# Turning the first half of the gated mixer sum by transposing DMAs in 16-bit halves, in place of TensorE transposes

## The chip, the core and the metric

The kernel runs on one core of one Trainium2 chip. The metric is the device time of one execution in microseconds (us), as the median of several runs. The core has five engines with queues of their own, which meet only through semaphores: TensorE (PE; its weight loads are shown as PEld), VectorE (DVE), ScalarE (ACT), GpSimd (POOL) and SyncE (SP). SP and POOL issue the transfers of this kernel, and an engine's instructions, issues included, run in the order of its own queue.

## The reference

It is an encoder of two layers over 512 tokens of 1024 channels, in float32. Each layer is a gated feed-forward half step, a mixer of two parallel branches, and a second feed-forward half step. The change touches the mixer's end:

```python
z = h @ w_in                                     # q, k, v, uf, ga, gf
y_na = neighbourhood_attention(q, k, v, rpb) @ w_na_out
y_f = fourier_mix(uf) @ w_f_out
g_na = jax.nn.sigmoid(ga + gate_bias[0])
g_f = jax.nn.sigmoid(gf + gate_bias[1])
return (g_na * y_na + g_f * y_f) @ w_o
```

The gated sum in brackets is 512 tokens x 1024 channels. To multiply it by `w_o`, the kernel needs it with channels on the partitions, while the gates produce it with tokens on the partitions. So it has to be turned.

## The kernel before

**Products.** Every large product is one Strassen step: both operands are cut in quarters, and seven products replace eight (numbered m; in the gate blocks their order is 1, 5, 2, 6, 7, 3, 4). Each float32 operand is split into a high part of few mantissa bits (`whi`, `xh`) and the rest (`wlo`, `xl`), and each product of two tiles is three matmuls: high by high, high by low, low by high (lines L491, L492, L494). A product works over two granules of weights (128 x 1024 float32, 512 KB each) and writes two PSUM banks (`A`, `B`, `C`), one for each 128 tokens. For each granule a raw load arrives by DMA (`raw`, L148 from SP's queue, L150 and L196 from POOL's queue, which add a second granule in memory), ScalarE rounds it to `whi` (L191, L186), and VectorE takes the difference `wlo` (L194, L187). Three buffers of `whi` and of `wlo` exist, so the rounding of a granule waits until TensorE has left the granule three before it. Eight granules are fetched ahead.

**Buffers.** In the mixer nearly all tiles of 4 KB a partition (raw weights, products taken out of PSUM, gated sums, turned tiles) come from one ring of 23 slots (`slot`, L111). A load into a slot waits for the last reader of the tile that was there.

**The gate blocks.** `gate_block(i, ...)` (L1371) computes both gates for column half i (512 of the 1024 channels) and all tokens, in the order of `ORDER`, and adds both gated branches. After m = 1 and m = 5 the results are evicted from PSUM by ScalarE (`snap`, L561, tile `sn`, one instruction for each bank); after m = 6 the product in the banks of `A` is evicted a second time, and m = 7 adds into the same two banks. A dictionary `after` names a function that is called behind a product. Block 0 leaves its sum in `ga0`, two tiles (j = 0, 1, 256 tokens each) of two token blocks of 512 channels. Block 1 runs next; it needs nothing of `ga0`, and its dictionary calls the turning of `ga0`, which is wanted only behind block 1 (`m00`, `m01`).

**Turning before the change.** `to_channels(i, ga, j)` (L1452) takes one tile in two steps. Each step makes four TensorE transposes of 128 x 128 float32 (L1459) into one PSUM bank and one ScalarE eviction (L1460) into the turned tile `mq`. It is called for j = 1 behind m = 5 and for j = 0 behind m = 2 of block 1, in each of the two layers; block 1's own sum is turned by the same function later and is not touched.

**A second way of turning that the kernel has.** The feed-forward stages turn their tile `z` of the same size by DMA (`halves` and `joined`, L676 to L698). A transposing DMA moves elements of 16 bits, so ScalarE first copies the low and the high 16-bit words into a tile `zs` (two copies, L681), one transposing DMA on SP's queue turns `zs` into `zt` (L682), and ScalarE later joins the words again into 32-bit elements (L698).

**Order of the queues.** A scheduler places the instructions of each engine by estimated times; in blocks under `manual_schedule` an engine keeps the order in which the code is written. In `gate_block` that is the case for ScalarE around the eviction behind m = 6:

```python
elif m == 6:
    product(pa, acts[6], K4, False, again=True)
    with tc.manual_schedule(engines={mybir.EngineType.Activation}):
        s2 = snap(pa)
        with_n(arg(s1, 0, 0), 0)
```

Of the kernel before, what the change touches and what calls it, by code (L numbers as in the profile page):

```python
# [9 lines left out]
F32 = mybir.dt.float32  # L10
# [3 lines left out]
U16 = mybir.dt.uint16  # L14
AF = mybir.ActivationFunctionType
# [3 lines left out]
P = 128  # L19
# [71 lines left out]
def encoder_kernel(  # L91
    ctx: ExitStack, tc: tile.TileContext, xin, xtr, wst, gains, gfin, gbias, bias_in, dft, chan, ident_in, rot, out
):
    nc = tc.nc
    V, S, G, PE = nc.vector, nc.scalar, nc.gpsimd, nc.tensor
# [11 lines left out]
    def nm(s):  # L107
        uid[0] += 1
        return f"{s}_{uid[0]}"

    def slot(dt=F32, s="k", shape=(4, 256)):  # L111
        return kp.tile([P, *shape], dt, tag="k", name=nm(s), bufs=23)
# [5 lines left out]
    def bank(s="ps"):  # L118
        return pp.tile([P, T], F32, tag="ps", name=nm(s))

    def pair(s="ps"):
        return [bank(s), bank(s)]
# [208 lines left out]
    def rsqrt(ms, n):  # L331
# [6 lines left out]
            V.scalar_tensor_tensor(r, t, 1.5, r, ALU.add, ALU.mult)  # L338
        return r

    class Norm:


# [214 lines left out]
    def snap(ps):  # L558
        t = slot(F32, "sn", (2, T))
        for b in range(2):  # L560
            S.activation(t[:, b, :], ps[b], AF.Copy)  # L561
        return t

    def less(ps, t):
        for b in range(2):
            res = V.tensor_tensor(t[:, b, :], ps[b], t[:, b, :], ALU.subtract)  # L566
        return res

    def combos(norm, t4):


        norm.tiles(0)
        norm.tiles(1)
        raw, hx, lx = norm.raw, norm.h, norm.l
        acts = {1: (hx[0], lx[0], 0), 2: (hx[1], lx[1], 0), 3: (hx[1], lx[1], 256)}
        if t4:
            acts[4] = (*t4, 0)

        def combine(m):
            p, a, b, op = {  # L580
                5: ((0, 0), (0, 0), (0, 1), ALU.subtract),
                7: ((0, 1), (0, 1), (1, 1), ALU.subtract),
                6: ((0, 0), (1, 1), (0, 0), ALU.add),
                4: ((1, 0), (1, 0), (0, 0), ALU.subtract),
            }[m]
            V.tensor_tensor(raw[p], raw[a], raw[b], op)
            yield
            if m != 4 or not t4:
                acts[m] = (slot(F32R, f"t{m}h"), slot(F32R, f"t{m}l"), 0)
            h, l, _ = acts[m]  # L590
            S.activation(h, raw[p], AF.Copy)
            yield
            V.tensor_tensor(l, raw[p], h.bitcast(F32), ALU.subtract)
            yield

        return acts, combine

    def stage_ffn(norm, nxt, late):
# [4 lines left out]
        def at_tile(h, j, c):  # L603
            if (h, j, c) not in at:
                at[h, j, c] = slot(F32, "at")
            return at[h, j, c]
# [35 lines left out]
        acts, steps_of = combos(norm, t4)  # L642
# [6 lines left out]
        if first:  # L649
            for g in range(2):  # L650
                w = ws.next()
# [22 lines left out]
        late_at, turned = [], []  # L674

        def halves(z, j, f0):  # L676

            s, t = slot(U16, "zs", (2, 4, 2, P)), slot(U16, "zt", (2, 4, 256))
            words = z.bitcast(U16).rearrange("p b (q f h) -> p h q b f", q=4, h=2)
            for h in range(2):  # L680
                S.activation(s[:, h], words[:, h], AF.Copy)  # L681
            nc.sync.dma_start_transpose(  # L682
                out=t.rearrange("p h q (b t) -> p (h q b) t", b=2), in_=s.rearrange("p h q b f -> p (h q b f)")
            )
            turned.append((t, j, f0))

        def joined():

            t, j, f0 = turned.pop(0)
            q = 0  # L690
            while q < 4:
                h, c, i = PLACE[f0 + q]
                n = 1
                while q + n < 4 and PLACE[f0 + q + n] == (h, c, i + n):
                    n += 1
                to = at_tile(h, j, c).bitcast(U16).rearrange("p i (t w) -> p w i t", w=2)
                for w in range(2):
                    S.activation(to[:, w, i : i + n, :], t[:, w, q : q + n, :], AF.Copy)  # L698
                q += n

        def plain_out():
# [161 lines left out]
        for jb in range(0 if first else 1, NB):  # L863
            f0 = 2 + 4 * jb
            if first and jb == 0:
                with tc.manual_schedule(engines={mybir.EngineType.DVE, mybir.EngineType.Activation}):
                    pa = pair("A")
                    product(pa, acts[1], K4, True)
                    for j in range(2):
                        t = snap(pcl[j])  # L870
# [13 lines left out]
            if turned:  # L884
                joined()
# [149 lines left out]
    def stage_mixer(l, norm, nxt):  # L1035
# [181 lines left out]
        def four_ch(b):  # L1217
            bh, bl = b
            p1, p2 = bank(), bank()
            mm3(p1[:, 0:258], ch[:, 0, 0, :], ch[:, 0, 1, :], bh[:, 0:258], bl[:, 0:258], True, True)  # L1220
            mm3(p2[:, 0:256], ch[:, 1, 0, :], ch[:, 1, 1, :], bh[:, 256:512], bl[:, 256:512], True, True)
            return p1, p2
# [27 lines left out]
        o, q, k, bms = [], {}, {}, {}  # L1250
# [120 lines left out]
        def gate_block(i, bias, acts, after):  # L1371

            r = norm.r

            def arg(src, which, j):
                t = src if src is not None else slot(F32, "ga", (2, T))
                for b in range(2):
                    c = 2 * j + b
                    V.scalar_tensor_tensor(
                        t[:, b, :], pa[b] if src is None else t[:, b, :], r[:, c : c + 1],  # L1380
                        bias[which][:, i * T : (i + 1) * T], ALU.mult, ALU.add,
                    )
                S.activation(t, t, AF.Tanh, scale=0.5)
                return t

            def gated(t, y):
                V.scalar_tensor_tensor(y, t, 1.0, y, ALU.add, ALU.mult)

            done = []

            def both(j):

                if j in done and (i, j) in ns:
                    V.tensor_tensor(fs[i, j], fs[i, j], ns[i, j], ALU.add)
                done.append(j)

            def with_f(t, j):
                gated(t, fs[i, j])
                both(j)

            def with_n(t, j):
                if (i, j) in ns:
                    gated(t, ns[i, j])
                    both(j)
                else:
                    ga[j] = t

            ga = [None, None]
            for m in ORDER:
                if m == 1:  # L1410
                    pa = pair("A")
                    product(pa, acts[1], K4, True)
                    s1 = snap(pa)
                elif m == 5:
                    pb = pair("B")
                    product(pb, acts[5], K4, True)
                    sb = snap(pb)
# [5 lines that stand above are left out]
                elif m == 2:  # L1423
                    pc = pair("C")
                    product(pc, acts[2], K4, True)
                    less(pc, s1)
                elif m == 7:
                    product(pa, acts[7], K4, False, again=True)
                    less(pa, sb)
                    with_f(arg(sb, 1, 1), 1)  # L1430
                elif m == 3:
                    product(pb, acts[3], K4, False, again=True)
                    less(pb, s2)
                    with_n(arg(s2, 0, 1), 1)
                else:
                    product(pa, acts[4], K4, False, again=True)
                    with_f(arg(None, 1, 0), 0)
                if m in after:
                    after[m]()
            return ga if (i, 0) not in ns else [fs[i, 0], fs[i, 1]]  # L1440
# [9 lines left out]
        mq = {}  # L1450

        def to_channels(i, ga, j):  # L1452
            mq[i, j] = slot(F32, "mq")
            for q in range(2):
                tr = bank("tr").rearrange("p (a b) -> p a b", a=2)
                for k in range(2):
                    for b in range(2):
                        d = (2 * q + k) * P
                        PE.transpose(tr[:, k, b * P : (b + 1) * P], ga[j][:, b, d : d + P], ident)  # L1459
                S.activation(mq[i, j][:, 2 * q : 2 * q + 2, :], tr, AF.Copy)  # L1460
# [26 lines left out]
        with tc.manual_schedule(engines={mybir.EngineType.DVE, mybir.EngineType.Activation}):  # L1487
            with tc.manual_schedule(engines={mybir.EngineType.PE}):
# [29 lines left out]
                f0, f1 = four_ch(b_[0]), four_ch(b_[1])  # L1518
# [26 lines left out]
                for s in range(3):  # L1545
                    t = slot(F32, "vs", (T,))
# [134 lines left out]
        acts = {1: (hx[0], lx[0], 0), 2: (hx[1], lx[1], 0), 3: (hx[1], lx[1], 256), 4: (hx[0], lx[0], 256)}  # L1681
# [11 lines left out]
        with tc.manual_schedule(engines={mybir.EngineType.DVE, mybir.EngineType.Activation}):  # L1693
# [10 lines left out]
            w = [ws.next(), ws.next()]  # L1704
        for _ in fill(o, ns, 0, w):
            pass
        bias = []
# [20 lines left out]

        ga0 = gate_block(0, bias, acts, {1: third_parts, 6: fourth})

        ga1 = gate_block(1, bias, acts, {5: lambda: to_channels(0, ga0, 1), 2: lambda: to_channels(0, ga0, 0)})
        m00, m01 = mq[0, 0], mq[0, 1]
        a1 = parts(m00, "m1")
        a5 = combo(m00, m00, m01, ALU.subtract, "m5")
        w = [ws.next(), ws.next()]
# [233 lines left out]
```

## Time and profile before

| | |
|---|---|
| median of 3 runs | 1862.26 us (1861.38 to 1863.63) |
| profiled execution, its own time | 1859.98 us |
| its span on the core | 1858.2 us |
| mean granted clock of TensorE in it | 0.998 |
| instructions | 24666 |
| busy: TensorE / VectorE / ScalarE | 99% / 86% / 70% of the span |
| mean transfer over the span | 211 GB/s |

The second gate block lies at about 516 to 556 us of the span in the first layer and at about 1437 to 1476 us in the second.

The page gives, in this order: the busy time of each engine; the span in 40 slices; the DMA queues; the chain of work that ended last, followed back from the last instruction to whatever released each step; and the costliest groups of instructions. A row of the order of time has the start (us from the span's start), the length, the engine, the line of the kernel, the operation, the tiles (out<-in), the shape and the count. In brackets stands the idle time of the engine just before it and what ended that. Engine names with a q (SPq) are queue entries that issue transfers. Neighbouring matmuls overlap, so their pace is read from start to start and not from their lengths. A row of a view by tile has the least, median and greatest length in ns, and the first and last start.

### The profile page before, as it was taken

What the parts mean: (1) busy time and instruction counts of PE and PEld (TensorE: products, weight loads), DVE (VectorE), ACT (ScalarE), POOL (GpSimd) and SP (SyncE); (2) the same over time, 40 slices, a digit from 0 to 9 for tenths busy, and PEclk for the clock granted to TensorE, in tenths of its full rate; (3) what the DMA queues carried; (4) which work ended last, traced back from release to release, by engine and by line L of the source; (5) the groups of instructions that cost most, each with busy time, mean ns of one, the idle gap of its engine ahead of it and who ended that gap; (6) DMA issues with size and microseconds to landing.
All of it is one profiled execution on the core that took longest, in us unless ns stands there. A gap on an engine that the chain in (4) does not pass through costs nothing.

```text
span 1858.2 us, 24666 instructions
## 1 busy us (share of the span) xinstructions
PE 1843.7 (99%) x8894; PEld 1533.9 (83%) x8894; DVE 1606.6 (86%) x1950; ACT 1300.2 (70%) x1772; POOL 171.3 (9%) x210
## 2 busy tenths in 40 slices
PE   9999999999999999999999999999999999999997
PEld 7888888888888888888888888888888888888886
DVE  7878899786989987889998888997869899888899
ACT  6777875668665767777666778666676576777865
POOL 0001011100101000101001100101001101010010
PEclk9999999999999999999999999999999999999999
DMA  9898799942986788879889897989249867998794
GB/s 302 223 232 218 198 256 274 213 121 86 254 219 164 171 227 231 208 200 264 256 194 223 224 221 199 269 278 209 69 149 236 210 171 176 229 215 215 210 280 148
DMA packets 190139, 392.13 MB, mean 211 GB/s; under 512 B 95488, under 2 KB 95616, under 8 KB 190016
## 3 DMA queue, kind: packets, MB, share of 16 engines
q1 hardware_dynamic: 161344, 292.20, 49.8%
q0 software_dynamic: 28528, 98.33, 30.2%
q8 instruction: 70, 1.15, 0.3%
q14 instruction: 53, 0.43, 0.1%
q10 hardware_dynamic: 144, 0.02, 0.0%
HBM read 365.85 MB, written 2.11 MB: 198 GB/s over the span
## 4 chain that ended last, share of the span: by engine, by line
PE 97%; DVE 1%; ACT 1%; DMA 0%; issue 0%; SPq 0%; DVEq 0%
PE A L491 10%; PE A L492 10%; PE A L494 10%; PE o L492 7%; PE o L494 7%; PE o L491 7%; PE B L492 5%; PE B L491 5%; PE B L494 5%; PE ps L315 4%; PE ps L316 3%; PE ps L317 3%; PE C L492 3%; PE C L491 3%; PE C L494 3%; PE tr L396 1%
## 5 line engine op out<-in xcount | busy, mean ns | idle before, releaser
L194 DVE TENSOR_TENSOR wlo<-raw,whi 128x1024 fp32r<-128x1024 f32 (+1 forms) x534 | 632.4, 1194 | 172.2 <-ACT whi L191 170.9
L191 ACT ACTIVATE whi<-raw 128x1024 fp32r<-128x1024 f32 (+1 forms) x534 | 547.4, 1033 | 265.6 <-PE A L492 58.5
L150 POOL DMA_DIRECT2D raw<-in_wst_dram x166 | 144.2, 885 | 1335.0 <-DMA raw<-in_wst_dram 794.1
L164 DVE TENSOR_TENSOR raw<-raw,raw 128x1024 f32<-128x1024 f32 (+1 forms) x150 | 179.2, 1195 | 2.0
L492 PE MATMUL A<-whi,xl 128*128 128x512 f32 x400 | 155.9, 390 | 0.0
L491 PE MATMUL A<-whi,xh 128*128 128x512 f32 x400 | 155.8, 390 | 0.0
L698 ACT ACTIVATE at<-zt 128x1024 uint16<-128x1024 uint16 (+2 forms) x96 | 111.0, 1169 | 20.9 <-DMA zt<-zs 20.9
L186 ACT ACTIVATE whi<-raw 128x1024 fp32r<-128x1024 f32 (+1 forms) x83 | 85.8, 1035 | 49.6 <-issue 12.5
L494 PE MATMUL A<-wlo,xh 128*128 128x512 f32 x400 | 115.1, 389 | 0.0
L187 DVE SCALAR_TENSOR_TENSOR wlo<-raw,whi 128x1024 fp32r<-128x1024 f32 (+1 forms) x83 | 98.4, 1195 | 13.7 <-ACT whi L186 13.7
L494 PEld LDWEIGHTS A<-wlo,xh 128*128 128x128 f32 x400 | 75.1, 188 | 15.6
L491 PEld LDWEIGHTS A<-whi,xh 128*128 128x128 f32 x400 | 75.1, 188 | 15.4
L492 PEld LDWEIGHTS A<-whi,xl 128*128 128x128 f32 x400 | 75.2, 188 | 15.3
L722 ACT ACTIVATE th<-sn,rh 128x512 f32<-128x512 f32 x80 | 55.2, 716 | 37.7 <-DVE sn L566 36.8
L491 PE MATMUL C<-whi,xh 128*128 128x512 f32 x208 | 81.2, 390 | 0.0
L492 PE MATMUL B<-whi,xl 128*128 128x512 f32 x208 | 81.1, 390 | 0.0
L492 PE MATMUL C<-whi,xl 128*128 128x512 f32 x208 | 81.0, 390 | 0.0
L491 PE MATMUL B<-whi,xh 128*128 128x512 f32 x208 | 81.0, 390 | 0.0
L681 ACT ACTIVATE zs<-th 128x1024 uint16<-128x1024 uint16 x80 | 79.5, 1043 | 0.7 <-DVE th L729 0.7
L561 ACT ACTIVATE sn<-A 128x512 f32<-128x512 f32 x104 | 59.1, 585 | 24.9 <-PE A L494 24.9
L494 PE MATMUL B<-wlo,xh 128*128 128x512 f32 x208 | 59.9, 390 | 0.0
L494 PE MATMUL C<-wlo,xh 128*128 128x512 f32 x208 | 59.8, 390 | 0.0
(438 smaller groups left out, 4676.5 us busy)
## 6 DMA issues: line engine op xcount, KB each, us to landing
raw<-in_wst_dram SPq DMA_DIRECT2D x470, 512.0 KB, 5.8
raw<-in_wst_dram POOLq DMA_DIRECT2D x174, 512.0 KB, 7.9
raw<-in_wst_dram SPq DMA_DIRECT2D x30, 256.0 KB, 4.1
bm<-in_bias_dram SPq DMA_DIRECT2D x16, 384.0 KB, 3.5
x<-in_xin_dram SPq DMA_DIRECT2D x4, 512.0 KB, 10.2
raw<-in_wst_dram POOLq DMA_DIRECT2D x8, 256.0 KB, 8.2
dft<-in_dft_dram POOLq DMA_DIRECT2D x8, 256.0 KB, 4.5
gb<-in_gbias_dram SPq DMA_DIRECT2D x4, 512.0 KB, 15.6
```

Of the source, the lines that this page charges most:

```text
L150: G.dma_start(out=self.t, in_=wst[GRAN_AT[self.plus]][:, 0 : self.n], accum_op=ALU.add)
L164: V.tensor_tensor(self.raw.t, self.raw.t, self.add.t, ALU.add)
L186: S.activation(hi, t, AF.Copy, scale=-1.0)
L187: self.last = V.scalar_tensor_tensor(lo, t, -1.0, hi.bitcast(F32), ALU.mult, ALU.subtract)
L191: S.activation(hi[:, cs], t[:, cs], AF.Copy)
L194: self.last = V.tensor_tensor(lo[:, cs], t[:, cs], hi[:, cs].bitcast(F32), ALU.subtract)
L315: PE.matmul(ps, lh, rh, start=start, stop=False, skip_group_check=again)
L491: PE.matmul(ps, lh, rh, start=start, stop=False, skip_group_check=again)
L492: PE.matmul(ps, ll, rh, start=False, stop=False, skip_group_check=again)
L494: PE.matmul(ps, lh, rl, start=False, stop=stop, skip_group_check=again)
L681: S.activation(s[:, h], words[:, h], AF.Copy)
L698: S.activation(to[:, w, i : i + n, :], t[:, w, q : q + n, :], AF.Copy)
```

## The change

The body of `halves` becomes a function `apart` and the joining of words becomes `joined_words`; the feed-forward stages call them with the same work as before. In the second gate block of the mixer, `ga0` is turned with them. Behind m = 1 the tile j = 1 is split and its transposing DMA issued, behind m = 5 the tile j = 0. Behind m = 2 the words of j = 1 are joined into `mq`, and behind m = 7 those of j = 0. The 2 x 8 TensorE transposes and 2 x 2 evictions of each layer go; 2 x 2 splitting copies, 2 transposing DMAs and 2 x 2 joining copies of each layer come. Two tiles for each turned tile, `zs` and `zt`, take slots of the ring.

In the built program the rest keeps its order on each engine but for a few neighbours in the block. The splits stand on ScalarE between and behind the two evictions of m = 1 and of m = 5, ahead of the weights. The first copy of the second join stands between the two evictions behind m = 6, the second behind the next weight rounding. On TensorE the first granule of m = 7 takes both banks' high-weight matmuls first and the low-weight ones behind them; before, the first bank's two low-weight matmuls stood between. On SP the two transposing DMAs have two weight loads between them. On VectorE the sum of two raw granules and the last addition of block 0 move ahead of one `wlo`.

```diff
+    def apart(z):
+
+        s, t = slot(U16, "zs", (2, 4, 2, P)), slot(U16, "zt", (2, 4, 256))
+        words = z.bitcast(U16).rearrange("p b (q f h) -> p h q b f", q=4, h=2)
+        for h in range(2):
+            S.activation(s[:, h], words[:, h], AF.Copy)
+        nc.sync.dma_start_transpose(
+            out=t.rearrange("p h q (b t) -> p (h q b) t", b=2), in_=s.rearrange("p h q b f -> p (h q b f)")
+        )
+        return t
+
+    def joined_words(to, t):
+
+        to = to.bitcast(U16).rearrange("p i (t w) -> p w i t", w=2)
+        for w in range(2):
+            S.activation(to[:, w], t[:, w], AF.Copy)
...
-        ga1 = gate_block(1, bias, acts, {5: lambda: to_channels(0, ga0, 1), 2: lambda: to_channels(0, ga0, 0)})
+        turned = {}
+
+        def taken(j):
+            turned[j] = apart(ga0[j])
+
+        def channels(j):
+            mq[0, j] = slot(F32, "mq")
+            joined_words(mq[0, j], turned[j])
+
+        ga1 = gate_block(
+            1, bias, acts, {1: lambda: taken(1), 5: lambda: taken(0), 2: lambda: channels(1), 7: lambda: channels(0)}
+        )
```

More of the change, by code (lines that the diff above doesn't have):

```diff
@@ L676, in halves @@
         def halves(z, j, f0):
[L678 to L685, printed above, removed]
+            turned.append((apart(z), j, f0))
         def joined():
@@ L695, in joined @@
                     n += 1
-                to = at_tile(h, j, c).bitcast(U16).rearrange("p i (t w) -> p w i t", w=2)
-                for w in range(2):
-                    S.activation(to[:, w, i : i + n, :], t[:, w, q : q + n, :], AF.Copy)
+                joined_words(at_tile(h, j, c)[:, i : i + n, :], t[:, :, q : q + n, :])
                 q += n
```

## The prediction

> **What bounds the kernel now.** First the page: the span, the busy shares, the chain that ended last. Then the tile that the removed transposes write, then the order of time of TensorE and ScalarE in the second gate block of the first layer, then the waits and stretches around it.
>
> ```profile
> span 1858.2 us, 24666 instructions
> PE 1843.7 (99%) x8894; PEld 1533.9 (83%) x8894; DVE 1606.6 (86%) x1950; ACT 1300.2 (70%) x1772; POOL 171.3 (9%) x210
> ...
> PE 97%; DVE 1%; ACT 1%; DMA 0%; issue 0%; SPq 0%; DVEq 0%
> ```
>
> TensorE is busy in 99% of the span and carries 97% of the chain. So an instruction taken off TensorE is worth its whole pace, and anything added elsewhere costs only what it makes TensorE wait. The view of stretches for the block in both layers (us busy and number of instructions of TensorE, its weight loads, VectorE, ScalarE and GpSimd, then granted clock, DMA share and GB/s):
>
> ```profile
> 521.00:528.00 7.00, 7.00 (x34) 5.78 (x34) 7.00 (x7) 4.77 (x7) 0.00 (x0) 1.00 0.29 82
> 528.00:534.00 6.00, 6.00 (x31) 5.00 (x30) 4.96 (x6) 3.24 (x6) 1.67 (x2) 1.00 0.97 264
> ...
> 521.00:556.00 35.00, 35.00 (x163) 29.00 (x163) 29.11 (x31) 21.93 (x27) 3.44 (x4) 1.00 0.82 212
> 1441.00:1476.00 35.00, 35.00 (x163) 29.00 (x162) 29.12 (x32) 21.78 (x27) 3.44 (x4) 1.00 0.78 213
> ```
>
> TensorE has no gap in either layer, at full granted clock. The second layer repeats the first (163 matmuls and 27 ScalarE instructions in 35 us in each), so I cost one layer and double it. ScalarE has 13 us free of 35. The DMA engines are at 0.29 up to 528 and at 0.97 behind it.
>
> **What the removal is worth.** The order of time on TensorE around the two groups of eight transposes:
>
> ```profile
> 527.16 0.62 PE L494 MATMUL B<-wlo,t1h 128*128 128x512 f32 x2
> 527.62 1.04 PE L1459 MATMUL tr<-ident,fs 128*128 128x128 f32 x8
> 528.41 0.48 PE L491 MATMUL C<-whi,xh 128*128 128x512 f32 x1
> 528.73 0.40 PE L492 MATMUL C<-whi,xl 128*128 128x512 f32 x1
> ...
> 533.50 0.62 PE L494 MATMUL C<-wlo,xh 128*128 128x512 f32 x2
> 533.96 1.03 PE L1459 MATMUL tr<-ident,fs 128*128 128x128 f32 x8
> 534.75 0.48 PE L491 MATMUL A<-whi,t2h 128*128 128x512 f32 x1
> 535.06 0.39 PE L492 MATMUL A<-whi,t2l 128*128 128x512 f32 x1
> ```
>
> The pace of the products is 0.23 us (two matmuls from 527.16 to 527.62). A group costs its own 0.79 us (527.62 to 528.41), and the product's first matmul behind it takes 0.32 us in place of 0.23. That is 0.88 us a group, the second one the same (0.79 and 0.31). Two groups in each of two layers: 4 x 0.88 = **3.54 us** off the path. These are all 32 transposes of the change.
>
> **What is added, and where it stands.** Each of the two tiles now takes two ScalarE copies into 16-bit halves, one transposing DMA on SP's queue, and two ScalarE copies that join the words, in place of two ScalarE evictions. The same steps stand in the feed-forward stages, on tiles of the same size, so they have prices:
>
> ```profile
> L681 ACT ACTIVATE zs<-th x80: 1035/1042/1063, 70.6 to 1748.8; 128x1024 uint16<-128x1024 uint16 x80
> L698 ACT ACTIVATE at<-zt x96: 477/1358/1386, 83.7 to 1767.1; 128x1024 uint16<-128x1024 uint16 x64, 128x256 uint16<-128x256 uint16 x16, 128x768 uint16<-128x768 uint16 x16
> L682 SPq DMA_TRANSPOSE zt<-zs x40: 1359/3700/7223, 72.6 to 1750.3; - x40
> DMA to landing us min/median/max: 4.3/5.9/10.1
> L1460 ACT ACTIVATE mq<-tr x16: 578/592/604, 528.8 to 1495.8; 128x512 f32<-128x512 f32 x16
> ```
>
> ScalarE gains 4 x 1.04 + 4 x 1.36 - 4 x 0.59 = 7.2 us in each layer, against 13 us free: it fits, if nothing urgent stands behind. ScalarE now, in order of time (tiles: whi the rounded weights, sn the products taken out of PSUM):
>
> ```profile
> 521.44 0.58 ACT L561 ACTIVATE sn<-A 128x512 f32<-128x512 f32 x1
> 521.97 1.06 ACT L191 ACTIVATE whi<-raw 128x1024 fp32r<-128x1024 f32 x1
> 533.75 1.06 ACT L191 ACTIVATE whi<-raw 128x1024 fp32r<-128x1024 f32 x1 [2.11 <-PE C L492]
> 539.12 0.60 ACT L561 ACTIVATE sn<-A 128x512 f32<-128x512 f32 x1 [1.21 <-PE A L494]
> 540.03 1.06 ACT L191 ACTIVATE whi<-raw 128x1024 fp32r<-128x1024 f32 x1 [0.31 <-PE A L492]
> 541.00 0.58 ACT L561 ACTIVATE sn<-A 128x512 f32<-128x512 f32 x1
> ```
>
> In the changed program the order is: sn, zs, sn, zs, whi, whi, sn, zs, sn, zs, whi, whi, both copies of the first join, whi, whi, sn, a copy of the second join, sn, the gate's tanh, whi, the last copy. I lay them end to end from 521.44, at 0.53 us from an eviction's start to the next step's (521.44 to 521.97) and 0.97 for a copy of 1.04 or 1.06 us (540.03 to 541.00). The splits end at 524.5 and 529.5, and the transposes are issued there. The weights that now start at 521.97 start at 524.4 and are ready at 525.5. They belong to the product that starts at 528.41 and will start at 527.5, so 2 us are left, and TensorE loses **nothing**. Without that cover it would lose up to the 2.4 us by which they moved. The first join stands at 531.3 to 533.9 and asks for a landing within 6.8 us of the issue. It starts while the DMA engines are at 0.29, where the range's lower half, 4.3 to 5.9, fits. Behind it stand the weights now at 533.75, wanted at 540.28 less 1.77, 538.5. They start at 533.9 and have 3.5 us left: **nothing** again.
>
> **The place that costs.** The second join's first copy stands between the two evictions of the product for m = 6, and the next product, m = 7, writes the same two banks again:
>
> ```profile
> 540.28 0.39 PE L491 MATMUL A<-whi,t3h 128*128 128x512 f32 x1
> ...
> 541.19 0.62 PE L494 MATMUL A<-wlo,t3h 128*128 128x512 f32 x2
> 541.64 0.48 PE L491 MATMUL A<-whi,t3h 128*128 128x512 f32 x1
> 541.96 0.40 PE L492 MATMUL A<-whi,t3l 128*128 128x512 f32 x1
> ```
>
> Here TensorE already loses 0.09 us (541.64 to 541.96 where 0.23 is the pace), because its seventh matmul needs the bank that the eviction at 541.00 to 541.58 frees. In the changed program that matmul stands fifth: the two low-weight matmuls that filled the time are moved behind it. So the bank is wanted 0.45 us sooner. The same three ScalarE steps stand in a feed-forward block:
>
> ```profile
> 685.03 0.60 ACT L561 ACTIVATE sn<-A 128x512 f32<-128x512 f32 x1 [1.21 <-PE A L494]
> 685.52 1.36 ACT L698 ACTIVATE at<-zt 128x1024 uint16<-128x1024 uint16 x1
> 686.74 0.57 ACT L561 ACTIVATE sn<-A 128x512 f32<-128x512 f32 x1
> ```
>
> There the second eviction starts 1.71 us behind the first; here it is 1.88 now (539.12 to 541.00, with a weight copy between). It will end 1.71 + 0.57 = 2.28 us behind the first. The product starts 1.16 us behind the first (540.28 less 539.12), and its fifth matmul is due 0.91 us later, at 2.07. TensorE waits some 0.3 us, 0.09 of it paid already: 0.2 us in each layer, **+0.4 us**. From below this is zero; from above it is the 0.45 us twice, 0.9. I take the value of the feed-forward row, the same sequence.
>
> That holds if the second transpose has landed at 539.12 + 0.49 - 1.77 = 537.8, which is 8.3 us after its issue at 529.5. The median of 40 is 5.9 and the longest 10.1. I take it as in time. Otherwise each us beyond 8.3 stands on TensorE's path in full, as ScalarE waits in order with the eviction behind it.
>
> **SP, POOL and buffers.** SP waits for each split with weight loads behind it, and each transpose holds the queue for 3.7 us (median).
>
> ```profile
> 525.01 0.33 SPq L148 DMA_DIRECT2D raw<-in_wst_dram  x1
> 547.84 1.06 ACT L191 ACTIVATE whi<-raw 128x1024 fp32r<-128x1024 f32 x1 [1.20 <-PE B L492]
> 533.19 0.86 POOL L196 DMA_DIRECT2D raw<-in_wst_dram  x1 [1.37 <-DVE wlo L194]
> raw<-in_wst_dram SPq DMA_DIRECT2D x470, 512.0 KB, 5.8
> raw<-in_wst_dram POOLq DMA_DIRECT2D x174, 512.0 KB, 7.9
> 548.54 0.39 PE L491 MATMUL B<-whi,xh 128*128 128x512 f32 x1
> ```
>
> The load at 525.01 comes behind the first transpose, some 3 us later. Its weights are rounded at 547.84, so of 23 us the 5.8 us landing leaves 17: no cost. POOL's accumulating load at 533.19 lands at some 541.1; TensorE wants those weights at 548.54, in the changed kernel at 546.8, and the rounding 1.06 us sooner, so the landing may slip 4.6 us. By how much two more transfers among full DMA engines delay it no row shows: from below nothing, from above one transpose's 5.9 us, 1.3 us too late in each layer, 2.6 us in all. I take nothing, as the first transpose runs in the idle stretch. The four more buffers of the ring take their places from tiles that are done, and PSUM is relieved by four banks: nothing.
>
> **The sum.** -3.54 + 0.4 = -3.1 us. The profiled execution took 1859.98 us (span 1858.2), 2.28 below the median of 1862.26, so a run like it would take 1856.9, and the median becomes **1859.1 us**. That is 0.17%; the bound that I use, 0.2%, is 3.7 us and about what a measurement of this kernel can tell from no change, so the likeliest outcome is a small gain inside it.
>
> **The rivals.** *The hand-over costs nothing:* the scheduler's fifth matmul finds its bank free, and the full 3.54 us show: 1858.7. For it speaks that the wait is 0.3 us, within the roughness of my clockwork; against it that the wait exists already.
>
> *The second transpose lands late:* 8.3 to 10.1 us after its issue, as the longest in the row did. With the longest in both layers TensorE loses 2 x 1.8 us, and the time is 1862.7, no gain. For it speaks that it flies where the DMA share is 0.97. Against it: the feed-forward transposes fly among the same traffic, and the ScalarE waits for them are
>
> ```profile
> ACT at L698 <- DMA zt<-zs: 20.9, 12, 3.9
> ```
>
> 20.9 us in all, in 12 waits, at 40 transposes and none longer than 3.9 us.
>
> *Slower:* the same place, with the transpose later still. The time is 1859.1 + 2 x (landing - 8.3), so it passes 1866.0, 0.2% above the median, from a landing of 11.7 us. The row's longest is 10.1, so it takes a condition that 40 transposes did not meet.
> [...]
>
> *Weights late:* the accumulating load at its upper bound, 1859.1 + 2.6 = 1861.7.
>
> **Chances and range.** Forecast 0.48, free hand-over 0.26, late transpose 0.14, weights late 0.05, slower 0.07. The three runs spread 1.1 us about their median, and 1858.5 is the bound of faster: about a third of the forecast and half of the free hand-over lie under it, 0.30. Slower takes its own 0.07 and 0.05 from the tails of the two late cases: 0.12. Same is 0.58. The range goes from the free hand-over less the spread, 1857.6, to the late transpose, 1862.7. The forecast's own range is 1858.0 to 1860.2.
>
> **What would show it.** Right: TensorE's L1459 has 32 matmuls, not 64, and in the block the products follow at 0.23 us; the wait for sn at the fifth matmul of m = 7 is some 0.3 us; the joins wait little or not at all for their DMAs; both transposes land within 8.3 us. Wrong: a TensorE gap at m = 7 of 1 us or more with ScalarE waiting for zt ahead of it, or waits for weights in the products for m = 2, 7 or 3.

## The result, and the profile after

The changed kernel takes 1859.33 us (median of 18 runs), the kernel before 1862.43 us (18 runs beside it). The ratio is 0.9985, with a 95% interval of 0.9979 to 0.9992: 2.8 us less by the ratio, 3.1 by the two medians, and 1.5 to 3.9 by the interval. That is a gain, as the interval leaves out zero, and a small one: the ratio lies inside the 0.2% set as the bound of "same", while the interval reaches a little past it. Two more sets of the changed kernel, taken beside the experiments, gave 0.9981 (0.9973 to 0.9990) and 0.9985 (0.9976 to 0.9993).

The page of the kernel after, its span, busy shares and the chain that ended last:

```profile
span 1857.9 us, 24616 instructions
PE 1842.2 (99%) x8862; PEld 1530.1 (82%) x8862; DVE 1605.6 (86%) x1950; ACT 1311.2 (71%) x1780; POOL 171.3 (9%) x210
...
PE 88%; DVE 6%; DMA 2%; issue 2%; ACT 1%; SPq 0%; DVEq 0%; ACTq 0%
```

32 matmuls are gone (8862 for 8894); TensorE stays the bound at 99%. The profiled execution took 1859.64 us, 0.3 us less than the one of before: single executions scatter by more than the change is worth (1856.88 to 1864.56 us in the 18 runs). So the change is measured on the path itself: from TensorE's first matmul of m = 1 in the second gate block to the first of the output sum (the block), and from there to the first of the next stage (the part behind). The rows of the first layer, first the kernel before, then after (order of time, TensorE):

```profile
522.17 0.39 PE L491 MATMUL B<-whi,t1h 128*128 128x512 f32 x1
...
556.70 0.39 PE L315 MATMUL ps<-whi,o 128*128 128x512 f32 x1
...
609.76 0.39 PE L491 MATMUL A<-whi,xh 128*128 128x512 f32 x1
```

```profile
522.87 0.39 PE L508 MATMUL B<-whi,t1h 128*128 128x512 f32 x1
...
539.19 0.39 PE L508 MATMUL A<-whi,t3h 128*128 128x512 f32 x1
539.42 0.39 PE L509 MATMUL A<-whi,t3l 128*128 128x512 f32 x1
539.64 0.39 PE L508 MATMUL A<-whi,t3h 128*128 128x512 f32 x1
539.87 0.39 PE L509 MATMUL A<-whi,t3l 128*128 128x512 f32 x1
540.36 0.50 PE L508 MATMUL A<-whi,t3h 128*128 128x512 f32 x1
540.70 0.39 PE L509 MATMUL A<-whi,t3l 128*128 128x512 f32 x1
...
555.91 0.39 PE L315 MATMUL ps<-whi,o 128*128 128x512 f32 x1
...
609.28 0.39 PE L508 MATMUL A<-whi,xh 128*128 128x512 f32 x1
```

The block shrank from 34.53 to 33.04 us. The part behind it grew from 53.06 to 53.37. The same two lengths for every kernel, each from its own rows, in both layers:

| kernel | block, layer 1 / 2 | part behind, 1 / 2 | ratio of the times, 95% interval |
|---|---|---|---|
| before | 34.53 / 34.53 | 53.06 / 53.03 | |
| after, three profiles | 33.04 to 33.05, all six | 53.37 / 53.05, 53.29 / 53.31, 53.65 / 53.44 | 0.9985 [0.9979, 0.9992] |
| nothing turned | 32.75 / 33.33 | 53.06 / 53.04 | 0.9979 [0.9969, 0.9989] |
| no transposing DMA | 33.05 / 33.05 | 53.06 / 53.03 | 0.9983 [0.9974, 0.9992] |
| one half by DMA | 33.65 / 33.65 | 53.06 / 53.08 | 0.9990 [0.9981, 0.9999] |
| second join late | 32.75 / 33.09 | 55.19 / 54.45 | 1.0000 [0.9992, 1.0009] |
| second join early | 33.16 / 33.05 | 53.29 / 53.32 | 0.9988 [0.9979, 0.9997] |
| both splits early | 33.05 / 33.05 | 53.04 / 53.03 | 0.9990 [0.9981, 0.9999] |
| both splits and joins early | 39.52 / 38.27 | 53.05 / 53.04 | 1.0034 [1.0022, 1.0047] |
| second split late | 40.33 / 40.18 | 53.07 / 53.05 | 1.0070 [1.0057, 1.0084] |
| each transposing DMA twice | 46.87 / 45.21 | 53.39 / 53.94 | 1.0111 [1.0097, 1.0126] |

So in each layer the change gains 1.49 us in the block and gives back 0.31 behind it (mean of six, from 0.02 to 0.59), 2 x 1.18 = 2.4 us net. The runs' three ratios say 2.8 to 3.5, with intervals that hold it.

The views by tile of the kernel after: the PSUM tile that TensorE's transposes write (`tr`) and the turned words (`zt`), over the run and, in the last two lines, in the first layer's block alone (us 520 to 550):

```profile
L1467 PE MATMUL tr<-ident,sn x32: 270/272/273, 569.7 to 1494.1; 128*128 128x128 f32 x32
...
L347 SPq DMA_TRANSPOSE zt<-zs x44: 1357/3464/6830, 72.8 to 1749.5; - x44
L356 ACT ACTIVATE mq<-zt x8: 1353/1358/1377, 531.9 to 1464.9; 128x1024 uint16<-128x1024 uint16 x8
...
L347 SPq DMA_TRANSPOSE zt<-zs x2: 2054/2520/2987, 525.1 to 530.2; - x2
DMA to landing us min/median/max: 4.3/4.4/4.6
```

In the mixer 32 transposes are left of 64, and the two DMAs of the block landed in 4.3 and 4.6 us (4.3 to 4.8 in all twelve of the three profiles).

### The profile page after: what moved, and what is told of

It is laid out like the page before. It is cut to its first block, busy times and chain, and to the rows that moved or that the text cites. A ratio compares the mean times of both kernels' runs of the same rounds, so it can differ in the third digit from the quotient of the medians.

```text
span 1857.9 us, 24616 instructions
## 1 busy us (share of the span) xinstructions
PE 1842.2 (99%) x8862; PEld 1530.1 (82%) x8862; DVE 1605.6 (86%) x1950; ACT 1311.2 (71%) x1780; POOL 171.3 (9%) x210
## 4 chain that ended last, share of the span: by engine, by line
PE 88%; DVE 6%; DMA 2%; issue 2%; ACT 1%; SPq 0%; DVEq 0%; ACTq 0%
PE A L508 10%; PE A L511 10%; PE A L509 10%; PE B L509 5%; PE B L508 5%; PE B L511 5%; PE o L511 5%; PE o L509 5%; PE o L508 4%; PE ps L315 4%; PE ps L316 3%; PE ps L317 3%; PE C L508 3%; PE C L509 3%; PE C L511 3%
## 6 DMA issues: line engine op xcount, KB each, us to landing
x<-in_xin_dram SPq DMA_DIRECT2D x4, 512.0 KB, 10.2
```

## The experiments

In the edits below, `taken(j)` splits a tile and issues its transposing DMA, `channels(j)` joins it; the number ahead is the product m behind which the step is asked for. All edits are to the changed kernel.

**What the transposes are worth: nothing turned, and one half.**

```diff
-            1, bias, acts, {1: lambda: taken(1), 5: lambda: taken(0), 2: lambda: channels(1), 7: lambda: channels(0)}
+            1, bias, acts, {}
         )
+        mq.update({(0, j): ga0[j].rearrange("p b (q f) -> p (b q) f", q=2) for j in range(2)})
```

> Leaves out the turning of the first column half altogether: the mixer sums are used unturned, so the output is another one. No TensorE transposes, no transposing DMA, no extra ScalarE copies; this is the most that the change could ever give. Theory (32 transposes worth 0.88 us per group of eight, hand-over at m = 7 costs 0.28 us a layer more than before): TensorE's starts behind the block come 1.77 us sooner a layer than in the kernel before (the changed kernel: some 1.46), the loss at m = 7 is back at 0.1 us, the time is 3.5 us below the kernel before, 0.6 below the changed kernel. Rival (the transposing DMAs or the four extra ScalarE copies cost something elsewhere too): more than 1 us below the changed kernel. Rival (a group is worth less than 0.88): less than 3 us below the kernel before.

```diff
-            1, bias, acts, {1: lambda: taken(1), 5: lambda: taken(0), 2: lambda: channels(1), 7: lambda: channels(0)}
+            1, bias, acts, {1: lambda: taken(1), 2: lambda: (channels(1), to_channels(0, ga0, 0))}
```

> Turns one tile (the one whose transposes stood ahead of m = 5) by DMA and the other by TensorE as before. Theory: the pace behind m = 1 is unchanged and one group, 0.88 us a layer, is saved; the second join no longer stands between the evictions of m = 6, so the loss at m = 7 is 0.1 us as before: 0.88 us a layer, 1.8 us in all, below the kernel before. Rival (the gain is not in the groups but in something that both tiles share, such as the order of the weights): not half of the gain, but nearly all (2.9) or nearly none.

The first and the last row of the block, with one half turned by DMA (order of time, TensorE), and then with nothing turned:

```profile
522.44 0.39 PE L508 MATMUL B<-whi,t1h 128*128 128x512 f32 x1
...
556.10 0.39 PE L315 MATMUL ps<-whi,o 128*128 128x512 f32 x1
```

```profile
522.09 0.39 PE L508 MATMUL B<-whi,t1h 128*128 128x512 f32 x1
...
554.84 0.39 PE L315 MATMUL ps<-whi,o 128*128 128x512 f32 x1
```

With one group less the block is 33.65 us, 0.88 shorter than before in both layers: one group is 0.88 us, as the rows of before had said. The median is 1860.48 against 1862.33 us, 1.85 less. With both groups gone the first layer's block is 1.78 shorter, twice 0.88 to 0.02. In the second layer it lost 0.58 of that at m = 7 behind a late weight rounding, which the changed kernel did not do. The time, 1858.48 us, is 0.95 below the changed kernel beside it; the two intervals overlap, so no cost outside block and part behind is shown.

**What the hand-over at m = 7 costs: the second join late, and early.**

```diff
-   ... 2: lambda: channels(1), 7: lambda: channels(0)}
+   ... 2: lambda: channels(1), 4: lambda: channels(0)}
```

> The changed kernel with one number other: the second join is asked for after m = 4 instead of m = 7, by which ScalarE has both copies of it behind the gate's tanh instead of one between the two evictions of m = 6. Theory (the 0.37 us at m = 7 is the copy between the evictions): the loss falls to 0.1 us, TensorE's starts behind the block come 1.75 us sooner a layer than before, the time is 0.5 to 0.6 us below the changed kernel. Rival (the bank is late for another reason, the eviction itself): 0.37 stays, same time. Rival (the later join is wanted by VectorE and delays the products behind the block): some tenths of a us to 1 us slower than the changed kernel.

The loss at the bank went, as the theory has it: the first layer's block is 32.75 us, 0.29 shorter than with the copy between the evictions. (In the second layer it is 33.09: there the rounding between the evictions waited 0.64 us for its load.) But the rival holds for the rest of the way. Waits of the part behind (us 553 to 584), engine and line, what it waited for, us in total, times, longest:

```profile
PEld ps L316 <- DVE wlo L194: 0.9, 1, 0.9
PEld wC L509 <- DVE m2l L322: 0.9, 1, 0.9
PE wC L509 <- DVE m2l L322: 0.6, 1, 0.6
PE ps L316 <- DVE wlo L194: 0.5, 1, 0.5
```

Both copies now start at 556.1 us, behind three tanh steps of the gate, where the changed kernel has them at 538.5 and 545.2; VectorE gets `mq` later, and TensorE waits for VectorE's low halves: 2.1 and 1.4 us a layer given back, more than the 1 us expected at most. The whole gain is gone (ratio 1.0000).

```diff
-   ... 2: lambda: channels(1), 7: lambda: channels(0)}
+   ... 2: lambda: (channels(1), channels(0))}
```

> The second join is asked for right behind the first (after m = 2), so both its copies stand ahead of the evictions of m = 6 and none between them; it needs its landing (4.6 us after the issue at 530.15, 534.7 us) by 535.4. Theory (the hand-over is lost to the copy between the evictions): the wait at the second bank of m = 7 falls from 0.37 to 0.1 us; instead the first eviction of m = 6 comes about 1 us later (539.0 for 538.0) and the first bank is late by up to 0.4 us: together within 0.2 us a layer of the changed kernel. Rival (the join's place does not matter, only the eviction's own time): 0.37 us at the second bank stays.

Its order of time on TensorE at m = 7:

```profile
538.47 0.61 PE L511 MATMUL A<-wlo,t2h 128*128 128x512 f32 x2
539.04 0.50 PE L508 MATMUL A<-whi,t3h 128*128 128x512 f32 x1
...
540.08 0.62 PE L511 MATMUL A<-wlo,t3h 128*128 128x512 f32 x2
540.66 0.51 PE L508 MATMUL A<-whi,t3h 128*128 128x512 f32 x1
```

Where the changed kernel waits once, this one waits twice and less: 0.12 us at the first bank (539.04 where 538.92 is the pace) and 0.13 at the second, each with a first matmul 0.11 longer. The block comes out the same, 33.16 and 33.05 us. The copy between the evictions is the cause of the wait; moving it only moves the price.

**What the transposing DMAs cost elsewhere: left out, and issued sooner.**

```diff
+        if not turn:
+            return s.rearrange("p h q b f -> p h q (b f)")
         nc.sync.dma_start_transpose(
...
-            turned[j] = apart(ga0[j])
+            turned[j] = apart(ga0[j], False)
```

> Leaves the two transposing DMAs of the first column half out and joins the split words as they are, so the output is another one; the ScalarE copies, and the order of ScalarE and TensorE, are those of the changed kernel. Theory (the DMAs are hidden): the same time as the changed kernel to within 0.3 us, 0.37 us lost at m = 7 as there; the second accumulating load of GpSimd at 533.8 lands after some 8 us as in the kernel before, instead of 10.3, without a gain to TensorE. Rival (the transposes cost the path something through SP's queue or the DMA engines): 0.5 us or more below the changed kernel.

The block is 33.05 us as in the changed kernel. But the 0.31 us behind it are not given back: 53.06 and 53.03, as before. The second accumulating load took 10.0 us, not the 8 expected, and 10.3 in the changed kernel; it lands 12.2 us ahead of the output sum's first matmul (543.11 to 555.31) instead of 11.8 (544.10 to 555.91). What so little can do there, VectorE's waits tell. First the kernel before, then after, then this run, then the run below (order of time, all rows of VectorE from us 543 to 582 that have idle time before them):

```profile
543.99 1.23 DVE L194 TENSOR_TENSOR wlo<-raw,whi 128x1024 fp32r<-128x1024 f32 x1 [1.65 <-ACT whi L191]
567.56 1.23 DVE L187 SCALAR_TENSOR_TENSOR wlo<-raw,whi 128x1024 fp32r<-128x1024 f32 x1 [1.28 <-ACT whi L186]
```

```profile
545.29 1.23 DVE L194 TENSOR_TENSOR wlo<-raw,whi 128x1024 fp32r<-128x1024 f32 x1 [1.83 <-ACT whi L191]
```

```profile
544.31 1.23 DVE L194 TENSOR_TENSOR wlo<-raw,whi 128x1024 fp32r<-128x1024 f32 x1 [1.45 <-ACT whi L191]
```

```profile
566.41 1.23 DVE L187 SCALAR_TENSOR_TENSOR wlo<-raw,whi 128x1024 fp32r<-128x1024 f32 x1 [1.29 <-ACT whi L186]
```

In the kernel before, VectorE caught up and idled 1.28 us at 567.56. In the kernel after it has no idle time from 545.29 on, and its low halves reach TensorE 0.3 us late. Two rows of the kernel after show where both ends of that come from, ScalarE's rounding ahead of 545.29 (order of time) and the wait of TensorE's weight loads (waits of the part behind, us 553 to 584):

```profile
544.20 1.06 ACT L191 ACTIVATE whi<-raw 128x1024 fp32r<-128x1024 f32 x1 [1.99 <-DMA raw<-in_wst_dram]
...
PEld ps L316 <- DVE wlo L194: 0.3, 1, 0.3
```

The load lands at 544.10, ScalarE has waited 1.99 us for it, VectorE waits for ScalarE, and TensorE for VectorE. Missing idle time alone costs nothing: without the DMAs VectorE has none from 544.31 on either, and nothing is lost. What counts is when VectorE starts on this load's weights. Counted from the start of the block, in layer 1 and layer 2, that is 22.42 and 22.04 us in the first profile of the changed kernel, 22.36 and 22.38 in the second, 22.75 and 22.36 in the third. The part behind is longer there by 0.31 and 0.02, 0.23 and 0.28, 0.59 and 0.41 us. Without the DMAs VectorE starts at 22.05 and 21.37; the part behind is not longer, and in layer 2 VectorE has 0.66 us of idle time left. By these rows the loss begins between 22.05 and 22.36 us, and with the transposes VectorE starts past that in five of six blocks. (The shares of the chain don't tell this: VectorE has 6%, 2% and 3% in the three profiles of the changed kernel, and 4% in the run without the DMAs.)

```diff
-            1, bias, acts, {1: lambda: taken(1), 5: lambda: taken(0), 2: lambda: channels(1), 7: lambda: channels(0)}
+            1, bias, acts, {1: lambda: (taken(1), taken(0)), 2: lambda: channels(1), 7: lambda: channels(0)}
```

> Both splits are asked for after m = 1, so the second transpose can be issued about a us sooner and is further ahead of GpSimd's two accumulating loads; the evictions of m = 1 come some 3 us later, into banks wanted only 12 us behind. Theory (the transposes cost what they delay the accumulating loads, after which VectorE has no gap for 36 us): the second accumulating load lands after 9 us or less instead of 10.3, and up to 0.25 us a layer come back behind the block; time 0 to 0.5 us below the changed kernel. Rival (the later evictions delay VectorE): 0.2 us or more above the changed kernel.

The second accumulating load was issued 10.4 us behind the block's start (532.88 less 522.50; 10.9 in the changed kernel) and landed after 8.9 us. In the first layer VectorE has its 1.29 us again (0.23 in the second, where the load took 10.2 us), and the part behind is 53.04 and 53.03 us: on TensorE's path this version is 0.3 us a layer better than the changed kernel. The times can't tell the two apart (1860.12 against 1859.80 us beside it), so it isn't called faster. Its second transposing DMA took 9.2 us, 4.6 more than in the changed kernel, and landed at 537.67, half a us before its join at 538.15.

**What a late landing costs.**

```diff
-   ... 5: lambda: taken(0), 2: lambda: channels(1), 7: ...
+   ... 2: lambda: (channels(1), taken(0)), 7: ...
```

> The second tile's split is asked for after m = 2, behind the first join, so its transpose is issued some 4 us later (near 534 us instead of 530.15); the join stays between the evictions of m = 6, due at 538.5. Theory (every us by which the landing passes 538.5 stands on TensorE's path in full, as ScalarE waits in order): with a landing L the gap ahead of the fifth matmul of m = 7 is 0.37 + (L - 538.5) us; with L some 4.4 us after the issue at 534 it is 0.3 to 0.5 us, with a landing after 8 us 3.5 to 4 us more, twice. Rival (the slack is larger, as VectorE and ScalarE have other work to move up): no gap beyond 0.4 us though L passes 539.5.

The order of time on ScalarE and TensorE, then a stretch (busy time of TensorE, its weight loads, VectorE, ScalarE, GpSimd, then the granted clock, DMA share, GB/s):

```profile
537.20 0.60 ACT L578 ACTIVATE sn<-A 128x512 f32<-128x512 f32 x1 [1.20 <-PE A L511]
543.23 1.34 ACT L356 ACTIVATE mq<-zt 128x1024 uint16<-128x1024 uint16 x1 [5.43 <-DMA zt<-zs]
...
545.06 0.80 PE L508 MATMUL A<-whi,t3h 128*128 128x512 f32 x1 [5.63 <-ACT sn L578]
545.66 0.63 PE L509 MATMUL A<-whi,t3l 128*128 128x512 f32 x1
546.08 0.63 PE L508 MATMUL A<-whi,t3h 128*128 128x512 f32 x1
...
545.00:548.60 3.60, 3.54 (x8) 2.81 (x9) 1.23 (x1) 3.28 (x5) 0.86 (x1) 0.50 0.12 48
```

Issued at 534.11, the transpose landed after 9.1 us. ScalarE waited 5.43 us for it and TensorE 5.63 us for the eviction behind: the wait passes on nearly one to one, as the theory has it. Then comes something that it doesn't have: the eight matmuls behind the gap run at a granted clock of 0.50, 3.58 us (545.06 to 548.64) where the changed kernel's same eight take 1.95 (540.36 to 542.31). The block is 7.28 us longer than the changed kernel's, for a wait of 5.6.

```diff
+   {1: lambda: (taken(1), taken(0)), 5: lambda: channels(1), 2: lambda: channels(0)}
```

> Both splits after m = 1, the first join after m = 5, the second after m = 2: the two moves of the runs beside it together, with the first join out of the way before the second. Theory: as there, the second bank's wait 0.1 us, the first eviction of m = 6 about 1 us late, the accumulating load sooner; 0 to 0.6 us below the changed kernel. Rival (ScalarE is late with everything, 4 copies in a row): the weights of m = 2 wait and the time is above the changed kernel.

Here the second transpose took 9.2 us again and its join was due sooner: ScalarE waited 4.00 us (ready at 533.80, start 537.80), TensorE 3.69, and the block is 6.5 and 5.2 us longer than in the changed kernel, with the half clock again (0.50 from the gap's end at 542.7 to 548.9). Neither theory had that wait; the version is slower than the kernel before (1868.41 against 1862.30 us).

```diff
-        nc.sync.dma_start_transpose(
+        for _ in range(times):
+            nc.sync.dma_start_transpose(
...
-            turned[j] = apart(ga0[j])
+            turned[j] = apart(ga0[j], 2)
```

> Each of the two transposing DMAs of the first column half is issued twice onto the same tile, the second one of no use, so the DMA work and SP's time are doubled. Theory (in the changed kernel 3.8 us lie between the second landing and its join): if the two transposes of a tile run behind each other, the first tile is whole near 534 us (join due 531.9, weights behind it 3.5 us slack: no loss beyond some tenths) and the second near 538 to 543 us: loss at m = 7 of 0 to 4.5 us a layer, equal to the landing less 538.5, plus 0.37. Rival (DMA work is not hidden but costs as a share of the engines' time): loss spread over the weight loads behind, as waits for raw, with the accumulating loads landing later than 12 us.

The first tile's two landed at 529.16 and 535.12, near the expected 534. The second tile's first one took 18.4 us, and the accumulating load issued 0.4 us behind it took 17.8; both landed within 0.2 us of each other. The view of that transpose alone by tile, and ScalarE and TensorE behind it:

```profile
DMA to landing us min/median/max: 18.4/18.4/18.4
...
556.61 1.34 ACT L357 ACTIVATE mq<-zt 128x1024 uint16<-128x1024 uint16 x1 [15.12 <-DMA zt<-zs]
...
558.90 0.79 PE L509 MATMUL B<-whi,xh 128*128 128x512 f32 x1 [11.20 <-ACT whi L191]
```

The loss is one wait behind the join, 11.2 us, and then a granted clock of 0.50 for 4.8 us (558.9 to 563.7). So the theory's mechanism holds and its size does not (0 to 4.5 us expected), because the landing was not 538 to 543 us but 556.6. Of the rival, the late accumulating load was seen (17.8 us where it named over 12), but not a loss spread over later waits for raw weights.

Two runs of the changed kernel itself stand beside these; their expectations: 

> The changed kernel itself, beside the experiments on one chip. Both theories: 0.9985 of the kernel before (some 2.8 us less), with the fifth matmul of m = 7 in the second gate block 0.50 us behind the fourth (0.37 lost at the hand-over), both transposes landed 4.3 to 4.6 us after their issue.

> The changed kernel once more, as the measure for the three versions beside it: 2.5 to 3.5 us below the kernel before, the products of the gate block 1.49 us sooner a layer, some 0.25 us of that given back in the two stages behind it.

Both were met, but for two landings of 4.7 us in the second profile, where 4.6 was the most named, and for the given-back time in the third, 0.59 and 0.41 us where some 0.25 were named.

## Why the prediction was right, and where it was not

The forecast was 1859.1 us; the median is 1859.33. By its own steps:

- *32 transposes at 0.88 us each group of eight, 3.54 us:* right. One group alone gave 0.88 us in both layers, two groups 1.78.
- *ScalarE's 7.2 us more a layer are hidden:* right for the places laid out. In the profile after, the splits end at 525.1 and 530.1, the first join starts at 531.9 and the next weights at 534.4; set off by the 0.7 us by which this layer starts later, they are within 0.25 us of the forecast's 524.5, 529.5, 531.3 and 533.9. The joins wait for no DMA.
- *The hand-over at m = 7:* right in place and cause, a little too small in size. The fifth matmul comes 0.49 us behind the fourth, 0.26 over the pace, and is 0.11 longer: 0.37, against 0.09 before. Forecast 0.3, so +0.2 us a layer; measured 0.28, and 0.29 from the run with nothing turned. The rival that it is free is refuted: all six blocks have it.
- *The second transpose lands within 8.3 us:* right, 4.3 to 4.8 us. The price of a late one was too low. One to one holds nearly for the wait in two runs (5.43 us on ScalarE and 5.63 on TensorE, 4.00 and 3.69); in the third, where TensorE waits behind the join, it was 15.12 and 11.20. Behind the gaps of 3.7 us and more TensorE also ran at half clock for 3.3 to 6.2 us, so the formula for the late cases (each us beyond 8.3 counted once) is short: a wait of 5.6 us made the block 7.3 us longer, one of 3.7 made it 6.5. The rival of a late landing was nearer than its 0.14 looks: three edits of one line put it at 8.2 to 9.3 us, and a fourth, which moves only the join, at 6.3 in one layer.
- *SP's queue:* right, no cost seen. *GpSimd's accumulating load, taken as nothing:* the step that failed, by 0.31 us a layer, 0.6 in all. The load slipped (10.3 us to landing for 8.0) and stayed within the 4.6 us that TensorE's own need of those weights allows. But the loss was not at that product: ScalarE and then VectorE started on these weights later, and VectorE, whose only idle time in the following 23 us had been 1.28 us, was late with low halves for the output sum.
- *The sum:* by the path, -3.56 + 0.6 (hand-over) + 0.6 (VectorE late) = -2.4 us for the forecast's -3.1. The two missed terms are smaller than the scatter of a run, so the times agree with both. That the median came out within 0.2 us of the forecast is in part luck: the path accounts for 2.4 us of the 3.1 by which the medians differ.

That VectorE was the engine to ask could have been read from the profile before: its rows behind us 545 have one idle time, the 1.28 us at 567.56, and TensorE was to run 1.57 us ahead of it. The size could not: with nothing turned TensorE runs 1.78 us ahead in the first layer, without the DMAs 1.49, and neither gives anything back. It takes the late load as well.

The order on ScalarE decides whether the gain stays: the second join behind the gate's tanh steps gives all of it back, and the second split one product later costs over five times the gain (1875.0 us for 1859.4).

## What to carry to other kernels

Price work that is taken off the bounding engine by its pace in the order of time, and then let every other engine run that much sooner, with the loads that the change delays. Here VectorE, with 1.28 us of idle time in 23 us, followed TensorE's lead of 1.5 us without loss, but not a later load on top of it. Ask of each moved wait which instruction stands behind it in order on its engine; here one copy between two evictions cost 0.28 us, and the same join asked for behind three tanh steps 1.4 to 2.1. A transposing DMA that landed 4.6 us after its issue in one order, 3.8 us ahead of its join, took 9.2 us in another and came half a us ahead, from a cause that no run isolates: measure its landing in the very order in which it will stand.

## What the runs showed of the hardware that was not expected

- **A gap of 3.7 us on TensorE cost more than the gap.** In the three slower runs the gaps were 5.6, 11.2 and 3.7 us in the first layer and 4.9, 9.3 and 3.8 in the second; the blocks are 7.3, 13.8 and 6.5 us and 7.1, 12.2 and 5.2 us longer than the changed kernel's. Behind them the granted clock stood at 0.50 for 3.7, 4.8 and 6.2 us and for 5.0, 3.7 and 3.3 us, and the matmuls' pace at 0.43 us instead of 0.23. These blocks have no gap between 0.9 and 3.7 us, so from which length on it happens is not shown.
- **The landing of one and the same transposing DMA differs widely with the order around it.** The second one of the block landed in 4.3 to 4.8 us in all profiles of the changed kernel, in 8.2 to 9.3 us in three other orders (both layers of each), and in 18.4 and 17.8 us where it was issued 0.3 to 0.4 us ahead of an accumulating load. In the three others an accumulating load was issued 1.4 to 1.9 us before SP had done with issuing the transpose, or 0.4 us ahead of it; in the changed kernel one comes 0.4 to 0.7 us before SP is done. This is a coincidence of times in the traces, and one row doesn't fit: with the second join late, the load came 0.7 us before SP was done too, and the transpose landed after 6.3 us (4.8 in the second layer). No run moved the accumulating load alone, so whether it is the cause stays open.
- The second accumulating load took 8.0 us to landing in the first layer of the kernel before, 8.7 with nothing turned, 10.0 with the two transposes left out and 10.3 with them. In the second layer these are 8.4, 10.0, 9.3 and 9.9. So the transposes' own part is 0.3 and 0.6 us; the rest comes without them, by up to 1.6 us even with nothing turned, and was not taken apart.
